# A hybrid four-layer trunk on one core: the state space layer's key units, B matrices and first value split moved

## The chip, the core and the metric

The program runs on one core of one Trainium2 chip, in one launch. The metric is the device time of a run in microseconds. TensorE is called PE here, VectorE DVE, ScalarE ACT and GpSimd POOL; SP starts most of the transfers. 256 tokens of width 1024 pass through four layers in float32.

## The reference, cut to what matters

```python
for i in range(4):
    hn = rms_norm(h, mix_norm_g[i])
    t = (pool_mixer, stick_breaking_attention, s5_mixer)[i % 3](hn, ...)
    h = h + t
    h = h + memory_cross_attention(rms_norm(h, xa_norm_g[i]), rms_norm(mem, mem_norm_g[i]), wq, wkv, wo)
    h = h + conv_glu_ffn(rms_norm(h, ffn_norm_g[i]), w_up, conv_w, conv_b, w_down)
return rms_norm(h, final_norm_g)

# s5_mixer, layer 2: 64 groups of 16 channels, 64 complex states each
bu = einsum('bcgi,gpi->bcgp', u, b_bar)           # B
x_t = a_bar * x_{t-1} + bu_t                      # recurrence over 256 tokens
y = gelu(real(einsum('bcgp,gip->bcgi', x, c_mat)) + d * u)
val, gate = split(y @ w_glu, 2); return val * sigmoid(gate)
```

The keys and values of the cross-attention come from `mem`, which does not depend on the layers before it. Their products can therefore be placed anywhere ahead of the cross-attention, and the kernel uses them as filler for PE.

## The kernel before

Every float32 product is three matmuls of split operands (`mm3`): a weight is loaded as 1 MB into one of three buffers called `raw`, ACT casts it into a high part `whi` and DVE or POOL subtracts to get the low part `wlo`, in two halves each (`load`). Each tag `whi` and `wlo` has six buffers. A program that lays the instructions out (the framework's scheduler) sets each engine's order within the order of the code and the limits given by `behind`; each engine then runs its own list strictly in order, and so do the DMA lists of SP, ACT and POOL.

The state space layer (`s5_mixer`, layer 2) runs between the FFN of layer 1 and the cross-attention of layer 2:

1. The normed tokens `u` are made on DVE (columns 0 to 511) and ACT (512 to 1023), then rearranged by eight SBUF to SBUF transfers into `uc` (L960).
2. `uc` is copied into `ur` (L985), transposed on PE (L989), and copied out as `v` (L990).
3. Four groups of small matmuls with the B matrices `bl` (1 MB each, `land(0)` to `land(3)`) give `S` (L1003, L1007). PE transposes `S`, and ACT and DVE copy the result into `SX` (L1027, L1029).
4. The recurrence runs on DVE alone over eight steps of chunks, `k` from 0 to 7, four instructions a step (L1049 to L1056), then three carried blocks (L1060 to L1066) that need the table `tab8`, which POOL computes.
5. PE adds the short-range part `taps_u` (four groups, matrices `tu`, L1076) and the carried part `carry` (four groups, matrices `ou`, L1101, needs the finished `X`), then GELU, a transpose and the GLU projection.

The filler is a plan: key units `k0` to `k3` (48 matmuls of 256 columns each, four key units in all) and the two value halves `v0` and `v1` (48 matmuls of 512 columns each), placed at named points by `fill`. A unit `+k1` only starts its load, `k1` multiplies. In the kernel before, `k1` and `k2` stand between step 1 and 2, `k3` after step 3, `v0` beside the recurrence, one group of `taps_u`, and then `v1`, whose PSUM banks are those of `v0` and come free when DVE has subtracted `vl` from them. The code puts that subtraction behind recurrence step 7 (`self.late = steps[7:8]`).

Of the kernel before, what the change touches and what calls it, by code (L numbers as in the profile page):

```python
# [36 lines left out]
class Trunk:  # L37
# [268 lines left out]
            return src[:, :, T * u : T * (u + 1)], DC, T  # L306
        return src[:, 4 * h : 4 * h + 4, D + 512 * u : D + 512 * (u + 1)], 4, 512

    def early(self, kind, l, u, **kw):

        for h in range(1 if kind == "k" else 2):
            self.loaded[kind, l, u, h] = self.load(*self.unit(kind, l, u, h), **kw)

    def weights(self, *key):
# [28 lines left out]
    def v_parts(self, l, nh):  # L343

        if nh == 0:
            self.V = self.kv_pair("v", TT, D)
        hi, lo = self.mg
        ps = [self.bank(), self.bank()]
        for kh in range(2):
            w = self.weights("v", l, nh, kh)  # L350
            for tt in range(TT):
                for k in range(4):
                    c = 4 * kh + k
                    s = slice(tt * P, (tt + 1) * P)
                    self.mm3(ps[tt][:], (hi[:, c, s], lo[:, c, s]), w(k, slice(0, 512)), c == 0, c == DC - 1)
                    yield
        vh, vl = self.V
        with self.behind(*self.late):
            for tt in range(TT):
                s = slice(512 * nh, 512 * (nh + 1))  # L360
                self.split(vh[:, tt, s], vl[:, tt, s], ps[tt][:])

    def fill(self, where):

# [11 lines left out]
    def plan(self, at, l, units):  # L376
        for u in units.split():
            if u[0] in "()":
                f = lambda u=u: self.portion(u, l)
            elif u[0] == "+":  # L380
                f = lambda u=u: self.early(u[1], l, int(u[2]), eng=self.nc.gpsimd if u[3:] else None)
            else:
                f = lambda u=u: (self.k_unit if u[0] == "k" else self.v_half)(l, int(u[1]))
            self.todo.setdefault(at, []).append(f)
# [547 lines left out]
    def s5_mixer(self, l, sp):  # L932
        nc, a = self.nc, self.a
        bls = []

        def land(mm):
            pool, tag = ((self.kv, "vh"), (self.kv, "vl"), (sp, "X"), (self.raw, "raw"))[mm]
            bl = pool.tile([P, 2, 4, 2, 2, 64], F32, tag=tag, name="bl")
            nc.sync.dma_start(bl[:].rearrange("p m q x r k -> p m (q x r k)"), self.blD[:, 2 * mm : 2 * mm + 2, :])
            bls.append(bl)  # L940

        land(0)
# [1 line left out]
        for tt in range(TT):  # L944
            rs.append(self.rstd(self.ss[tt]))
        self.fill("u0")
        u = self.big.tile([P, TT, D], F32, tag="xs", name="u")
        uc = sp.tile([P, 8, 16, 16], F32, name="uc")
        chain, firsts = [], []
        for tt in range(TT):  # L950
            r = rs[tt]
            firsts = []
            for nh, f in enumerate((nc.vector.tensor_scalar_mul, nc.scalar.mul)):
                s = slice(512 * nh, 512 * (nh + 1))
                done = f(u[:, tt, s], self.h[:, tt, s], r[:, 0:1])
                firsts.append(done.ins)

            for q in range(4):
                at = 32 * q + 16 * tt
                last = nc.sync.dma_start(  # L960
                    uc[at : at + 16].rearrange("c t a j -> c t (a j)"), u[:, tt, 256 * q : 256 * (q + 1)]
                )
        chain.append(done.ins)
# [3 lines left out]
        with self.behind(last.ins):  # L967
            for i, row in enumerate((a["s5_d"][0], a["mix_norm_g"][l])):
                nc.sync.dma_start(db[:, i, :], bass.AP(tensor=row.tensor, offset=row.offset, ap=[[256, 4], [0, 32], [1, 256]]))
            land(1)  # L970
            land(2)
        with self.behind(self.powed):
            nc.gpsimd.tensor_mul(db[:, 0, :], db[:, 0, :], db[:, 1, :])
            tab8 = self.s5_eighths(sp)
        self.late = firsts
        self.fill("u")
        land(3)
        self.after = [chain, chain + [last.ins]]
        self.fill("u1")
        self.late = ()  # L980
# [28 lines left out]
        tus = []  # L1009

        def taps_land(mm):
            pool, tag = ((self.acts, "ah"), (self.raw, "raw"), (self.raw, "raw"), (self.raw, "raw"))[mm]
            tu = pool.tile([P, 2, 2, 4, P], F32, tag=tag, name="tu")
            tus.append(tu)
            return nc.sync.dma_start(tu[:].rearrange("p r m q k -> p r (m q) k"), self.tD[mm]).ins
# [23 lines left out]
        with self.behind(last.ins):  # L1039
            nc.scalar.preload_act_table_set("gelu_apprx_tanh_and_others")  # L1040
        tab = sc[:, 0 : 3 * GP].rearrange("p (x g) -> p x g", g=GP)
        steps = []
        for k in range(8):
            nb = 4 if k < 7 else 3
            cur = lambda r=1: X[:, ::r, :, k : 8 * nb : 8].rearrange("p x g b -> p x b g")
            new = X[:, :, :, k + 1 : 8 * (nb - 1) + k + 2 : 8].rearrange("p x g b -> p x b g")
            add = SX[:, k : 8 * nb : 8].rearrange("p b x g -> p x b g")
            if k == 0:
                steps.append(vec.tensor_copy(new, add).ins)  # L1049
                continue  # L1050
            pr = two[:].rearrange("p (n x b g) -> p n x b g", n=2, x=2, b=4)[:, :, :, 0:nb]
            sh = [P, 2, nb, GP]
            vec.tensor_mul(pr[:, 0], cur(), tab[:, 0:1, :].unsqueeze(2).to_broadcast(sh))
            vec.tensor_mul(pr[:, 1], cur(-1), tab[:, 1:3, :].unsqueeze(2).to_broadcast(sh))
            vec.tensor_add(new, pr[:, 0], add)
            steps.append(vec.tensor_add(new, new, pr[:, 1]).ins)  # L1056
        for b in range(1, 4):
# [4 lines left out]
            for r, t in ((1, tab8[:, 0:1]), (-1, tab8[:, 1:3])):  # L1062
# [1 line left out]
                vec.tensor_mul(pr, carried[:, ::r].unsqueeze(3).to_broadcast(sh), t[:, :, :, 0:n].to_broadcast(sh) if r > 0 else t[:, :, :, 0:n])  # L1064
                new = X[:, :, :, 8 * b + 1 : 8 * b + 1 + n]
                steps.append(vec.tensor_add(new, new, pr).ins)  # L1066
        self.late = steps[7:8]
        self.fill("scan0")

        Y = self.accs()  # L1070

        def taps_u(mm):
            with self.behind(self.multiplied):
                for m, par, q in [(m, par, q) for m in (2 * mm, 2 * mm + 1) for par in range(2) for q in range(4)]:
                    c0 = (m % 4) * P
                    nc.tensor.matmul(  # L1076
                        Y[2 * par + m // 4][32 * q : 32 * q + 32, c0 : c0 + P], v[:, 2 * m + par, 32 * q : 32 * q + 32], tus[mm][:, par, m % 2, q, :],
                        start=m % 4 == 0, stop=False, tile_position=(0, 32 * q), skip_group_check=True,
                    )

        self.late = steps[-1:]
        taps_u(0)
        self.fill("scan1")
        self.late = ()
        for mm in (1, 2, 3):
            landed = taps_land(mm)
            taps_u(mm)

# [195 lines left out]
    def run(self, layers=range(DEPTH), parts="mcf"):  # L1284
# [14 lines left out]
        for l in layers:  # L1299
            if "c" not in parts:  # L1300
                break
            if l == first or l % 3 == 0 and l - 1 not in layers:
                self.plan((l, "start"), l, "k0 k1 k2 k3")
                self.plan((l, "pool"), l, "+v0g")
                self.plan((l, "xnorm0"), l, "(v0.8")
                self.plan((l, "xnorm"), l, ").5")
                self.plan((l, "xnorm1"), l, ")")
                self.plan((l, "soft"), l, "v1")
            elif l % 3 == 1:
                self.plan((l, "xnorm"), l, "k0 k1 k2 (k3.10")  # L1310
                self.plan((l, "xnorm1"), l, ")")
                self.plan((l, "soft"), l, "v0 v1")
            elif l % 3 == 2:
                self.plan((l - 1, "fnorm"), l, "(k0.10")
                self.plan((l - 1, "fnorm1"), l, ")")
                self.plan((l, "u0"), l, "+k1 +k2")
                self.plan((l, "u"), l, "k1 k2")
                self.plan((l, "u1"), l, "+k3")
                self.plan((l, "s"), l, "k3 +v0g")
                self.plan((l, "scan0"), l, "v0")  # L1320
                self.plan((l, "scan1"), l, "+v1g v1")
            else:
                self.plan((l - 1, "soft"), l, "k0")
                self.plan((l - 1, "fnorm"), l, "(k1.10")
                self.plan((l - 1, "fnorm1"), l, ")")
                self.plan((l, "mnorm"), l, "k2 k3")
                self.plan((l, "pool"), l, "+v0g")
                self.plan((l, "xnorm0"), l, "(v0.8")
                self.plan((l, "xnorm"), l, ").5")
                self.plan((l, "xnorm1"), l, ")")  # L1330
                self.plan((l, "soft"), l, "v1")
# [13 lines left out]
        for m in range(8):  # L1345
            at = (5 * m) // 2 + 2
            put((1, f"up{at}"), lambda m=m: self.s5_powers(m))
            put((1, f"up{at + 2}"), lambda m=m: self.s5_taps(m))
            if m % 2:
                put((1, f"up{at + 4}") if m < 7 else (2, "start"), lambda m=m: self.s5_spread(m // 2))  # L1350

        for l in layers:
            self.layer = l
# [64 lines left out]
```

## Time and profile before

| | us |
|---|---|
| median of three runs | 1495.98 (1493.38 to 1496.36) |
| the profiled execution | 1494.25 |
| its span, first to last instruction | 1492.5 |
| PE busy in the span | 1426.9 (96%) |
| DVE busy | 1093.6 (73%) |
| ACT busy | 839.8 (56%) |
| POOL busy | 127.2 (9%) |

PE's share is an average over the whole span. The chain that ended last gives PE 76%, DVE 11% and DMA 7%. The state space layer up to the start of its GLU lies between about 775 and 871 us of the span.

### The profile page before, as it was taken

Reading aid. Unit: us, or ns where it says so; the run is one execution under the profiler, and the core shown is the slowest. Engines: PE = TensorE matmul, PEld = TensorE weight load, DVE = VectorE, ACT = ScalarE, POOL = GpSimd, SP = SyncE. Lnnn points to the kernel's source line nnn. Section 1 sums busy time; section 2 is a strip of 40 time slices with the busy share of each in tenths; the row PEclk is TensorE's granted clock in tenths of the full one; section 3 lists DMA queues with packets and bytes.
Section 4 is the critical chain, followed back from the end, with each engine's and each line's share of the span. In section 5 each row is a group of like instructions: output and inputs, shape, how many; then the busy total and the mean of one; then the engine's idle time right before and its main releaser. Section 6 shows DMA issues by size and latency. Waiting matters only on the chain.

```text
span 1492.5 us, 25390 instructions
## 1 busy us (share of the span) xinstructions
PE 1426.9 (96%) x10354; PEld 1317.2 (88%) x10354; DVE 1093.6 (73%) x1720; ACT 839.8 (56%) x1351; POOL 127.2 (9%) x128
## 2 busy tenths in 40 slices
PE   7999999999999999999997679999999999999997
PEld 7897999988998989999986558999999999899996
DVE  6869887867886668978773646767767776677775
ACT  6654655547885556545544145656555565465553
POOL 3401000000000000101125100000000030000000
PEclk9999999999999999999998889999999999999999
DMA  7667656635444545766669383556555554465551
GB/s 253 229 166 222 221 202 204 215 127 190 142 150 156 198 149 197 233 218 227 220 192 275 139 270 130 172 170 219 170 188 180 174 204 145 142 225 171 182 185 43
DMA packets 205682, 279.75 MB, mean 187 GB/s; under 512 B 23740, under 2 KB 163132, under 8 KB 203644
## 3 DMA queue, kind: packets, MB, share of 16 engines
q1 hardware_dynamic: 199420, 263.08, 53.4%
q0 software_dynamic: 6144, 15.04, 3.1%
q8 instruction: 81, 1.33, 0.4%
q14 instruction: 37, 0.30, 0.1%
HBM read 264.24 MB, written 16.94 MB: 188 GB/s over the span
## 4 chain that ended last, share of the span: by engine, by line
PE 76%; DVE 11%; DMA 7%; ACT 3%; issue 2%; SPq 1%; POOL 0%; DVEq 0%; POOLq 0%; ACTq 0%
PE u L66 9%; PE u L67 9%; PE u L65 9%; PE mm L65 7%; PE mm L66 7%; PE mm L67 7%; PE acc L65 7%; PE acc L66 7%; PE acc L67 7%; DMA raw<-in_ffn_w_up_dram 3%; DVE wlo L71 3%; DVE ug L1256 1%; ACT whi L70 1%; DMA bl<-blD 1%; DVE h L434 1%
## 5 line engine op out<-in xcount | busy, mean ns | idle before, releaser
L71 DVE TENSOR_TENSOR wlo<-raw,whi 128x1024 fp32r<-128x1024 f32 x428 | 517.1, 1221 | 156.3 <-ACT whi L70 148.2
L70 ACT CAST whi<-raw 128x1024 fp32r<-128x1024 f32 (+1 forms) x450 | 460.0, 1045 | 192.6 <-DMA raw<-in_ffn_w_up_dram 58.2
L65 PE MATMUL u<-ah,whi 128*128 128x256 f32 x1408 | 400.3, 285 | 1.9 <-DVE ug L1256 1.4
L66 PE MATMUL u<-al,whi 128*128 128x256 f32 x1408 | 399.9, 284 | 0.7 <-DVE al L71 0.7
L67 PE MATMUL u<-ah,wlo 128*128 128x256 f32 x1408 | 399.6, 284 | 0.0
L65 PEld LDWEIGHTS u<-ah,whi 128*128 128x128 f32 x1408 | 271.1, 193 | 6.4 <-issue 2.8
L66 PEld LDWEIGHTS u<-al,whi 128*128 128x128 f32 x1408 | 271.3, 193 | 3.6 <-DVE al L71 1.1
L67 PEld LDWEIGHTS u<-ah,wlo 128*128 128x128 f32 x1408 | 271.3, 193 | 0.0
L1256 DVE SCALAR_TENSOR_TENSOR ug<-u,cwT,ug 128x255 f32<-128x255 f32 x352 | 168.6, 480 | 99.6 <-ACT ug L1254 94.4
L1254 ACT ACTIVATE ug<-u,cwT 128x256 f32<-128x256 f32 x176 | 99.0, 562 | 183.7 <-PE u L67 122.7
L65 PE MATMUL acc<-whi,gg 128*128 128x512 f32 x352 | 138.0, 392 | 0.0
L66 PE MATMUL acc<-wlo,gg 128*128 128x512 f32 x352 | 137.9, 392 | 0.0
L67 PE MATMUL acc<-whi,gg 128*128 128x512 f32 x352 | 136.9, 389 | 0.0
L66 PE MATMUL mm<-al,whi 128*128 128x256 f32 x384 | 109.3, 285 | 0.1
L65 PE MATMUL mm<-ah,whi 128*128 128x256 f32 x384 | 109.1, 284 | 0.0
L67 PE MATMUL mm<-ah,wlo 128*128 128x256 f32 x384 | 108.8, 283 | 0.0
L176 POOL TENSOR_TENSOR r<-v,mhalf 128x1 f32<-128x1 f32 x28 | 22.0, 788 | 826.8 <-DVE v L172 678.2
L67 PEld LDWEIGHTS acc<-whi,gg 128*128 128x128 f32 x352 | 66.1, 188 | 14.4
L65 PEld LDWEIGHTS acc<-whi,gg 128*128 128x128 f32 x352 | 66.4, 189 | 11.7
L66 PEld LDWEIGHTS acc<-wlo,gg 128*128 128x128 f32 x352 | 66.4, 189 | 10.7
L65 PE MATMUL acc<-whi,ah 128*128 128x512 f32 (+1 forms) x192 | 73.0, 380 | 1.9 <-ACT whi L70 1.7
L66 PEld LDWEIGHTS mm<-al,whi 128*128 128x128 f32 x384 | 73.9, 192 | 0.8 <-DVE al L71 0.6
(354 smaller groups left out, 2573.8 us busy)
## 6 DMA issues: line engine op xcount, KB each, us to landing
raw<-in_ffn_w_up_dram SPq DMA_DIRECT2D x88, 1024.0 KB
raw<-in_ffn_w_down_dram SPq DMA_DIRECT2D x44, 1024.0 KB
raw<-in_xa_wkv_dram SPq DMA_DIRECT2D x30, 1024.0 KB
raw<-in_xa_wq_dram SPq DMA_DIRECT2D x16, 1024.0 KB
raw<-in_xa_wo_dram SPq DMA_DIRECT2D x16, 1024.0 KB
raw<-in_sb_w_qkv_dram SPq DMA_DIRECT2D x12, 1024.0 KB
raw<-in_s_w_glu_dram SPq DMA_DIRECT2D x8, 1024.0 KB
raw<-in_sb_w_o_dram SPq DMA_DIRECT2D x4, 1024.0 KB
```

What stands on the lines that cost most here:

```text
L65: mm(out, lh, rh, start=start, stop=False)
L66: mm(out, lh, rl, start=False, stop=False)
L67: self.multiplied = mm(out, ll, rh, start=False, stop=stop).ins
L70: x = self.nc.scalar.copy(hi, src)
L71: y = (eng or self.nc.vector).tensor_sub(lo, src, hi.bitcast(F32))
L176: self.powed = nc.gpsimd.tensor_tensor(r[:], v[:], self.mhalf[:], ALU.pow).ins
L434: self.nc.vector.tensor_add(hs, hs, ps[:])
L1254: nc.scalar.activation(u[:, s, :], out, AF.Identity, bias=cw[3], scale=cw[2])
L1256: nc.vector.scalar_tensor_tensor(u[:, s, sh:], out[:, : T - sh], cw[2 - sh], u[:, s, sh:], ALU.mult, ALU.add)
```

## The change

`k3` is planned with `k1` and `k2`. B matrix 1 is loaded ahead of the tokens, and matrices 2 and 3 are started from POOL's list behind the two reciprocal roots `r`. Four of the eight `uc` transfers are started from ACT's list. The low part of the first half of `v0`'s weights goes from POOL to DVE. `taps_u(1)` is taken ahead of `v1`, with its matrix in a buffer of its own (tag `al`). `v0` is emitted inside the recurrence at `k == 7`, and the first multiply of step 7 is held behind the two `vl` subtractions. One scratch transfer (`s5_spread(3)`) is emitted later.

```diff
@@ early
+            kw.update({"eng": engs[h]} if engs else {})
@@ v_parts
-                self.split(vh[:, tt, s], vl[:, tt, s], ps[tt][:])
+                self.halved = self.split(vh[:, tt, s], vl[:, tt, s], ps[tt][:])[1:]
@@ s5_mixer
-        def land(mm):
+        def land(mm, eng=nc.sync):
-            nc.sync.dma_start(bl[:].rearrange("p m q x r k -> p m (q x r k)"), self.blD[:, 2 * mm : 2 * mm + 2, :])
+            eng.dma_start(bl[:].rearrange("p m q x r k -> p m (q x r k)"), self.blD[:, 2 * mm : 2 * mm + 2, :])
         self.fill("u0")
+        land(1)
-            for q in range(4):
+            for q in (2, 3, 0, 1):
-                last = nc.sync.dma_start(
+                last = (nc.sync if q < 2 else nc.scalar).dma_start(
-            land(1)
-            land(2)
         with self.behind(self.powed):
+            land(2, nc.gpsimd)
+            land(3, nc.gpsimd)
+            tab8 = self.s5_eighths(sp)
             nc.gpsimd.tensor_mul(db[:, 0, :], db[:, 0, :], db[:, 1, :])
-            tab8 = self.s5_eighths(sp)
         self.late = firsts
         self.fill("u")
-        land(3)
@@ taps_land
-            pool, tag = ((self.acts, "ah"), (self.raw, "raw"), (self.raw, "raw"), (self.raw, "raw"))[mm]
+            pool, tag = ((self.acts, "ah"), (self.acts, "al"), (self.raw, "raw"), (self.raw, "raw"))[mm]
@@ the recurrence
+            if k == 7:
+                self.fill("scan0")
+                half = self.halved
-            vec.tensor_mul(pr[:, 0], cur(), tab[:, 0:1, :].unsqueeze(2).to_broadcast(sh))
+            with self.behind(*half):
+                vec.tensor_mul(pr[:, 0], cur(), tab[:, 0:1, :].unsqueeze(2).to_broadcast(sh))
-        self.late = steps[7:8]
-        self.fill("scan0")
+        taps_land(1)
         self.late = steps[-1:]
         taps_u(0)
+        taps_u(1)
         self.fill("scan1")
-        for mm in (1, 2, 3):
+        for mm in (2, 3):
@@ the plan of layer 2
-                self.plan((l, "u0"), l, "+k1 +k2")
-                self.plan((l, "u"), l, "k1 k2")
-                self.plan((l, "u1"), l, "+k3")
-                self.plan((l, "s"), l, "k3 +v0g")
+                self.plan((l, "u0"), l, "+k1 +k2 +k3")
+                self.plan((l, "u"), l, "k1 k2 k3")
+                self.plan((l, "u1"), l, "+v0dg")
```

On DVE, inside the recurrence (steps 5 to 7; `vl` is the low part of the first value half, `two` and `X` are the recurrence), the kernel before has no subtraction here:

```order
L1056 TENSOR_TENSOR X<-X,two 128x2x4x32
L1053 TENSOR_TENSOR two<-X,sc 128x2x96
L1054 TENSOR_TENSOR two<-X,sc 128x2x96
L1055 TENSOR_TENSOR X<-two,SX 128x2x3x32
L1056 TENSOR_TENSOR X<-X,two 128x2x3x32
L1060 COPY sc<-X 128x64
L1064 TENSOR_TENSOR two<-sc,tab_8524 128x512
```

The changed kernel has both ahead of step 7:

```order
L71 TENSOR_TENSOR vl<-mm,vh 128x512
L1061 TENSOR_TENSOR X<-X,two 128x2x4x32
L1058 TENSOR_TENSOR two<-X,sc 128x256
L1059 TENSOR_TENSOR two<-X,sc 128x256
L1060 TENSOR_TENSOR X<-two,SX 128x2x4x32
L71 TENSOR_TENSOR vl<-mm,vh 128x512
L1061 TENSOR_TENSOR X<-X,two 128x2x4x32
L1058 TENSOR_TENSOR two<-X,sc 128x2x96
```

The two subtractions moved from the second carried block up into steps 5 and 6.

On ACT, from the tokens `u` on, the kernel before has this list (`kh` casts a key unit, `whi` a weight, `ur`, `v`, `S`, `SX` as in the steps above):

```order
L955 ACTIVATE u<-h,r 128x512 x2
L70 CAST kh<-mm 128x512 x2
L70 CAST whi<-raw 128x1024 x2
L985 COPY ur<-uc 128x512 x2
L990 COPY v<-mm 128x512 x2
L1007 COPY S<-mm 128x512 x2
L70 CAST whi<-raw 128x1024 x4
L70 CAST kh<-mm 128x512
L1029 COPY SX<-mm 128x8x32
```

In the changed kernel the same place reads:

```order
L957 ACTIVATE u<-h,r 128x512 x2
L962 DMA uc<-u 16x8x256 x4
L70 CAST kh<-mm 128x512 x3
L986 COPY ur<-uc 128x512 x2
L991 COPY v<-mm 128x512
L70 CAST whi<-raw 128x1024 x2
L991 COPY v<-mm 128x512
L1008 COPY S<-mm 128x512
L70 CAST whi<-raw 128x1024 x2
L1008 COPY S<-mm 128x512
L1030 COPY SX<-mm 128x8x32
```

The casts of the first value half's two weights moved from behind the two copies of `S` to between the copies of `v` and of `S`, and the third `kh` moved ahead of `ur`.

On PE, where the second value half begins, the kernel before has one group of taps and then a run on one bank, `mm_9013`, with twelve matmuls before the second bank `mm_9014`:

```order
L1076 MATMUL acc2_8975<-tu_8836,v_8662 32x128 x4
L65 MATMUL mm_9013<-whi_8995,mgh_6215 128x512
L66 MATMUL mm_9013<-wlo_8996,mgh_6215 128x512
L67 MATMUL mm_9013<-whi_8995,mgl_6216 128x512
L65 MATMUL mm_9013<-whi_8999,mgh_6215 128x512
```

The changed kernel has a second group of taps (`tu_8973`), and then both banks at once:

```order
L1080 MATMUL acc0_8975<-tu_8973,v_8733 32x128 x4
L1080 MATMUL acc2_8977<-tu_8973,v_8733 32x128 x4
L65 MATMUL mm_9031<-whi_9013,mgh_6215 128x512
L65 MATMUL mm_9032<-whi_9013,mgh_6215 128x512
L66 MATMUL mm_9031<-wlo_9014,mgh_6215 128x512
```

The second matmul of `v1` now writes the second bank, so it needs both subtractions `vl`, not only the first.

## Rows read from the trace of the kernel before

**Rows 1.** The page: the span, and the group of low-part subtractions on DVE.
```profile
span 1492.5 us, 25390 instructions
...
L71 DVE TENSOR_TENSOR wlo<-raw,whi 128x1024 fp32r<-128x1024 f32 x428 | 517.1, 1221 | 156.3 <-ACT whi L70 148.2
```

**Rows 2.** Waits of PE, 770 to 935 us: total us, times, longest.
```profile
PE mm L65 <- DVE vl L71: 11.5, 1, 11.5
PE acc L1101 <- DMA ou<-caD: 5.8, 2, 2.9
PE mm L989 <- ACT ur L985: 4.8, 1, 4.8
PE mm L1003 <- DMA bl<-blD: 3.9, 2, 2.5
```

**Rows 3.** Windows: engines' busy us, granted PE clock, DMA share, GB/s (the last three).
```profile
780.00:790.00 10.00, 6.55 (x55) 6.35 (x53) 3.23 (x4) 3.06 (x4) 5.33 (x11) 1.00 1.16 124
790.00:797.00 7.00, 5.54 (x48) 4.67 (x48) 2.66 (x5) 2.33 (x5) 0.00 (x0) 0.52 1.00 352
...
839.50:845.00 5.50, 5.49 (x13) 4.33 (x14) 5.21 (x9) 0.00 (x0) 0.00 (x0) 0.52 0.00 0
```

**Rows 4.** Timeline of PE from uc to v0: start, us, line, count [idle before].
```profile
791.37 3.67 PE L989 MATMUL mm<-ident,ur 128*128 128x128 f32 x16 [4.82 <-ACT ur L985]
...
799.40 1.08 PE L1003 MATMUL mm<-bl,v 128*32 128x128 f32 x32 [2.49 <-DMA bl<-blD]
801.92 3.64 PE L1003 MATMUL mm<-bl,v 128*32 128x128 f32 x64 [1.44 <-DMA bl<-blD]
...
812.12 1.47 PE L1027 MATMUL mm<-ident,S 128*128 128x128 f32 x12
...
815.56 1.01 PE L65 MATMUL mm<-whi,mgh 128*128 128x512 f32 x2 [0.83 <-ACT SX L1029]
```

**Rows 5.** Timeline of PE from the first taps to the GLU.
```profile
826.95 1.08 PE L1076 MATMUL acc<-tu,v 128*32 128x128 f32 x32
839.51 0.79 PE L65 MATMUL mm<-whi,mgh 128*128 128x512 f32 x1 [11.48 <-DVE vl L71]
...
855.83 1.35 PE L1101 MATMUL acc<-ou,X 64*32 64x128 f32 x64
860.03 1.16 PE L1101 MATMUL acc<-ou,X 64*32 64x128 f32 x64 [2.85 <-DMA ou<-caD]
864.13 3.67 PE L1101 MATMUL acc<-ou,X 64*32 64x128 f32 x128 [2.94 <-DMA ou<-caD]
...
870.93 0.50 PE L65 MATMUL mm<-whi,ah 128*128 128x512 f32 x1 [1.65 <-ACT ah L1121]
```

**Rows 6.** Timeline of DVE: the recurrence.
```profile
816.05 0.42 DVE L1049 COPY X<-SX 128x256 f32<-128x256 f32 x1 [0.68 <-ACT SX L1029]
...
831.20 0.59 DVE L1055 TENSOR_TENSOR X<-two,SX 128x256 f32<-128x256 f32 x1
...
838.77 0.68 DVE L71 TENSOR_TENSOR vl<-mm,vh 128x512 fp32r<-128x512 f32 x1
...
844.30 0.62 DVE L1066 TENSOR_TENSOR X<-X,two 128x448 f32<-128x448 f32 x1
```

**Rows 7.** Timeline of ACT: the uc copies, and the casts of v0's second weight.
```profile
790.70 1.14 ACT L985 COPY ur<-uc 128x512 f32<-128x512 f32 x2 [1.63 <-DMA uc<-u]
...
807.21 2.00 ACT L70 CAST whi<-raw 128x1024 fp32r<-128x1024 f32 x2 [0.69 <-DMA raw<-in_xa_wkv_dram]
```

**Rows 8.** Timeline of POOL: d times uc, and one low part.
```profile
799.13 4.51 POOL L992 TENSOR_TENSOR uc<-uc,db 128x2048 f32<-128x2048 f32 x1
...
805.64 2.39 POOL L71 TENSOR_TENSOR wlo<-raw,whi 128x1024 fp32r<-128x1024 f32 x1 [1.58 <-PE mm L1003]
```

**Rows 9.** Timeline of SP: the uc transfers, and v0's two weights.
```profile
778.04 5.45 SPq L960 DMA_DIRECT2D uc<-u  x8
...
786.47 4.45 SPq L88 DMA_DIRECT2D raw<-in_xa_wkv_dram  x2
```

More of the change, by code (lines that the diff above doesn't have):

```diff
@@ L307, in unit, with early @@
         return src[:, 4 * h : 4 * h + 4, D + 512 * u : D + 512 * (u + 1)], 4, 512
-    def early(self, kind, l, u, **kw):
+    def early(self, kind, l, u, engs=(), **kw):
         for h in range(1 if kind == "k" else 2):
+            kw.update({"eng": engs[h]} if engs else {})
             self.loaded[kind, l, u, h] = self.load(*self.unit(kind, l, u, h), **kw)
@@ L380, in plan @@
             elif u[0] == "+":
-                f = lambda u=u: self.early(u[1], l, int(u[2]), eng=self.nc.gpsimd if u[3:] else None)
+                f = lambda u=u: self.early(u[1], l, int(u[2]), engs=[None if c == "d" else self.nc.gpsimd for c in u[3:].replace("g", "gg")])
             else:
@@ L1041, in s5_mixer @@
         tab = sc[:, 0 : 3 * GP].rearrange("p (x g) -> p x g", g=GP)
-        steps = []
+        steps, half = [], ()
         for k in range(8):
@@ L1349, in run @@
             if m % 2:
-                put((1, f"up{at + 4}") if m < 7 else (2, "start"), lambda m=m: self.s5_spread(m // 2))
+                put((1, f"up{at + 4}") if m < 7 else (2, "u1"), lambda m=m: self.s5_spread(m // 2))
         for l in layers:
```

## The prediction

> **What bounds the kernel now.** The page comes first: in a span of 1492.5 us [rows 1] PE is busy 96%, so a time that goes must be a time in which PE waits. The list of PE's waits, cut to the state space layer, shows them: 11.5 us for `vl` on DVE, 5.8 us in two waits for `ou`, 4.8 us for the rearranged tokens, 3.9 us for `bl` [rows 2], 26.0 us together. The reader should then look at the clock in the windows: it is 0.52 (so mostly the lower level, 1.2 GHz) in 790 to 797 us and again in 839.5 to 845 us, both times directly behind one of these waits [rows 3]. So a long wait is paid twice, once as idle time and once in slow matmuls behind it. The timelines say which step holds the layer. From 791.37 us on it is one chain: transposes, B groups, `k3`, transposes of `S` from 812.12 us, and DVE's recurrence from 816.05 us [rows 4, 6]. I call that start of the recurrence R and count from it. PE does `v0` and one group of taps until 828.0 us (826.95 + 1.08), then waits for the first `vl`, which stands late in DVE's list, until 839.51 us, R + 23.5 [rows 5, 6]. The carried part starts at 855.83 us, R + 39.8, and the GLU at 870.93 us, R + 54.9 [rows 5]. Behind the GLU nothing in the change moves, so I take its start as the finish line: what it gains, the run gains.
>
> **Up to R.** `k3` goes ahead of the tokens' transposes. It removes the 6.6 us between the B groups' end (801.92 + 3.64 = 805.56 us) and 812.12 us [rows 4], and fills the wait of 4.82 us ahead of 791.37 us: `k1` and `k2`, twice as many matmuls, ran for 11.6 us up to 786.55 us (791.37 - 4.82), so `k3` takes 5.8 us and PE is busy to 792.4 us. Ahead of `u`, two more low parts of 1.22 us each [rows 1] stand in DVE's list, and two more casts of 1.0 us [rows 7] on ACT ahead of the norm's squares. They run side by side, so I put `u` 2.2 us later: its transfers start at about 780.2 us, not 778.04 us [rows 9].
>
> Then the transfers. Before, `uc` was first started at 778.04 us and had all landed at 790.70 us [rows 7, 9], with the DMA share at 1.16 but only 124 GB/s moved from 780 to 790 us [rows 3]. I read that as engines full with small pieces, about 9.5 us of work for `uc`. Starting half of them from ACT saves issue time (5.45 us for eight on SP [rows 9]; four on each side take 2.7 us), but the engines were already full, and the two B matrices that POOL now starts at the same moment add to their work. If two rings halved the time of `uc`, it would land at 786 us or so; that belongs to the quick case below. The Trainium skill speaks against that case, in "DMA: Bandwidth & Descriptors", section "Issuing engines are not separate DMA queues": transfers started from several engines end up on the same 16 DMA engines and interleave there, and only the issue time is saved. The share of 1.16 agrees with it; by that rule `uc` saves nothing beyond the 2.7 us of issue.
>
> So I sum the DMA work from 780.5 us: `uc` 9.5 us, then at 352 GB/s [rows 3] the two matrices (2.1 MB, 6.0 us), one scratch copy (0.5 MB, 1.5 us) and `v0`'s first weight (1.05 MB, 3.0 us): that weight lands at about 800.5 us. `uc` is somewhere within, at 791 to 795 us, and PE waits 1 to 3 us for it behind `k3`, not 4.8.
>
> The cost is in ACT's list: the two casts of that weight now stand between the first and the second copy of `v`, so the third B group waits for a weight that PE needs only ten microseconds later. Casts 2.0 us, copy 0.6 us: 803.1 us. Groups three and four took 3.64 us after a wait and will again [rows 4]: 806.8 us. The second weight's casts (landing near 803.5 us) fit in beside them. From the transposes of `S` to R it was 816.05 - 812.12 = 3.9 us [rows 4, 6]; I add 0.5 us for the low clock. **R = 811.2 us, 4.8 us earlier.** Bounds: 806.5 us, where no cast waits for its transfer (k units to 792.4, copies 0.6, transposes 3.7, four groups 1.1 each, 2.0 us of casts, 3.9 us), and 816 us or later, where the weight lands 5 us later than I sum. I take the value between, because 807.21 us, the landing of `v0`'s second weight before, is the nearest row [rows 7] and the sum of the work is nearly the same.
>
> **From R to the GLU.** The `vl` subtractions now stand in steps 5 and 6. PE's list has the second bank in its second matmul of `v1`, so the later `vl` counts. The instruction that it follows began at 831.20 us and took 0.59 us, R + 15.7 [rows 6]; the first `vl` ahead of it adds 0.6 us, instructions that run beside PE's work a little slower than this one 0.3 us (my estimate), and the second is 0.68 us [rows 6]: R + 17.3. PE finishes `v0` at R + 11 and two groups of taps (1.08 us each [rows 5]) at R + 13, so a wait of 4.3 us stays of the 11.5. It is about as long as the one ahead of 791.37 us, behind which the clock was low, so I keep `v1` at its old length: from 839.51 us to 855.83 us are 16.3 us, less three groups of taps at 1.08 us, 13.1 us. Two groups are left behind it, 2.2 us. The carried part can start at R + 32.6, not R + 39.8. DVE's recurrence itself ends as before, at R + 28.9 (844.30 + 0.62 us [rows 6]), since the subtractions were inside it then as well. So it is not the next bound.
>
> The carried part has four groups of 1.35 us. Before, two `ou` matrices waited for buffers that `taps_u` 1 and 2 held; now only one does, that of the third group of taps, free at R + 31.5. The first of the two late ones before came 6.3 us behind its buffer (second taps over at 855.83 - 2 x 1.08 = 853.7, use at 860.03 us [rows 5]). So: groups one and two until R + 35.3, wait to R + 37.8, groups three and four until R + 40.5, then as before 3.1 us to the GLU (870.93 - 864.13 - 3.67 us [rows 5]): R + 43.6 against R + 54.9. **Gain 11.3 us.** Bounds: with no low clock in `v1` (as `v0`, 826.95 - 815.56 = 11.4 us [rows 4, 5]) and an `ou` landing without a wait, 4.2 us more; with the recurrence held up by POOL, less. POOL's list is the one that got longer ahead of DVE's need. The table `tab8` now ends behind both weights' low parts (2.39 us each), `d * uc` (4.51 us) and `v1`'s four low parts [rows 8]: from the cast of `v0`'s second weight 6 x 2.4 + 4.5 + about 7 us of small work = 26 us, some 832 us, and DVE needs it at about R + 21.5 = 832.7 us. It just fits; each microsecond more moves the recurrence's end, which has 32.6 - 28.9 = 3.7 us of slack to PE.
>
> **Sum.** 4.8 + 11.3 = 16.1 us. Against the profiled execution, whose own time is 1494.25 us (the span and 1.75 us around it), that gives 1478.2 us. The median shown, 1495.98 us, is 1.7 us higher, 1479.9 us on that base; I say **1479 us**.
>
> **The rivals.**
>
> *Quick transfers.* `uc` and `v0`'s first weight land before they are asked for, `v1` runs at full clock, and the last `ou` is there in time. R = 806.5 (9.5 us gained), 11.3 and 4.2 us more: 25.0 us, 1469 us. For it: two rings may overlap the gaps of the small pieces. Against it: a share above 1 leaves little room.
>
> *The cast stall eats the first part.* ACT holds the third B group until a weight that lands 5 us later than I sum, R stays at 816 us, and only the second part is left: 1494.25 - 11.3 = 1483 us. For it: five transfers now crowd into the same ten microseconds. Against it: before, the same bytes were through at 807 us.
>
> *Given back.* The GLU's weights set the pace from there, since their buffers are freed by `tu` and `ou`, and the earlier start is waited for later: no change, 1492 to 1496 us. Against it: these buffers come free earlier by as much as the GLU starts earlier.
>
> *Slower.* If the large pieces from POOL's queue share the engines at the pace of the small ones, 124 GB/s [rows 3], then the 5 MB up to `v0`'s first weight last 40 us, it lands at 821 us, R becomes 832 us (10.7 us behind it, as in the forecast), and the GLU starts at 875.6 us, 4.7 us later: 1499 us. This turns the balance from the point at which the weight lands later than 816.5 us. For it: 10 us at that pace are in the trace. Against it: from 790 us on, with POOL's copies and the weights mixed, 352 GB/s were moved.
>
> **How the numbers follow.** Forecast (1474 to 1483 us) 0.50, quick transfers 0.18, cast stall 0.18, given back 0.06, slower 0.07, something else 0.01. The range that leaves out no more than 2 in 10 reaches from a little below the quick case to some way beyond the cast stall: 1468 to 1488 us; the forecast's own is 1474 to 1483 us. A measurement of this kernel tells 0.2% (3 us) from no change, as its three runs lie 3 us apart. Faster: 0.50 + 0.18 + 0.18 and a little of "given back", 0.87; same 0.06; slower 0.07.
>
> **What would show it.** PE's wait for `vl` should fall from 11.5 to about 4 us, the waits for `bl` should be gone, and one wait for `ou` of some 2.5 us should be left. R should lie at 807 to 814 us, with ACT waiting for `raw<-in_xa_wkv` between the two copies of `v`. DVE should show no wait for POOL at its first carried block; if it waits there by more than 4 us, the POOL estimate was wrong. If R has moved but the GLU's start has not, the step "R to the GLU" failed; if the GLU starts earlier and the time stays, "nothing behind it moves" failed.

## The result, and the profile after

The changed kernel takes **1481.02 us** (median of 4 runs, 1480.47 to 1482.43), the kernel before 1494.68 us in the same comparison: a ratio of 0.992, 95% interval 0.9901 to 0.9939. The forecast was 1479 us, its range 1468 to 1488 us. The profiled span fell from 1492.5 us [rows 1] to 1480.7 us, by 11.8 us; the medians lie 13.7 us apart.

The first view to read again is the list of PE's waits, 770 to 935 us (total us, times, longest):

```profile
PE mm L990 <- ACT ur L986: 5.2, 1, 5.2
PE mm L65 <- DVE vl L71: 4.4, 2, 2.4
PE acc L1106 <- DMA ou<-caD: 3.5, 1, 3.5
PE mm L65 <- ACT ah L1126: 3.1, 2, 1.7
PE mm L1004 <- ACT v L991: 2.2, 1, 2.2
PE acc L65 <- ACT whi L70: 1.6, 1, 1.6
...
PE acc L1106 <- issue: 0.4, 1, 0.4
```

Against [rows 2], `vl` fell from 11.5 to 4.4 us, `bl` is gone, `ou` fell from 5.8 to 3.5 us, with 0.4 us more ahead of the same matmuls for which the profile shows no releaser (`issue`). But the wait for the rearranged tokens is as long as before (5.2 us) although `k3` now fills 5.8 us ahead of it, and there is a new one for a copy of `v`. PE's timeline shows where these lie (start, us, count, idle before; x4, x19 and x43 count only what lies in a view's window); it answers to [rows 4, 5]:

```profile
775.16 0.28 PE L65 MATMUL mm<-mgh,whi 128*128 128x256 f32 x1
...
797.78 1.12 PE L990 MATMUL mm<-ident,ur 128*128 128x128 f32 x4 [5.18 <-ACT ur L986]
806.13 1.29 PE L1004 MATMUL mm<-bl,v 128*32 128x128 f32 x19 [2.21 <-ACT v L991]
...
830.90 0.80 PE L65 MATMUL mm<-whi,mgh 128*128 128x512 f32 x1 [2.44 <-DVE vl L71]
846.41 0.85 PE L1106 MATMUL acc<-ou,X 64*32 64x128 f32 x43
851.95 1.11 PE L1106 MATMUL acc<-ou,X 64*32 64x128 f32 x59 [3.50 <-DMA ou<-caD]
859.06 0.50 PE L65 MATMUL mm<-whi,ah 128*128 128x512 f32 x1 [1.68 <-ACT ah L1126]
```

The tokens' transposes start 6.4 us later than before, and yet R comes 2.7 us earlier, since `k3` and the waits for `bl` no longer lie behind them. On DVE, the recurrence (answering to [rows 6]) shows the two `vl` inside it, and `tab8`'s first use behind POOL's last step of it (both timelines: start, us, line):

```profile
813.35 1.22 DVE L1050 COPY X<-SX 128x256 f32<-128x256 f32 x1 [1.02 <-ACT SX L1030]
...
827.23 0.67 DVE L71 TENSOR_TENSOR vl<-mm,vh 128x512 fp32r<-128x512 f32 x1
830.17 0.68 DVE L71 TENSOR_TENSOR vl<-mm,vh 128x512 fp32r<-128x512 f32 x1
...
833.91 0.70 DVE L1069 TENSOR_TENSOR two<-sc,tab 128x512 f32<-128x512 f32 x1
```
```profile
832.42 0.87 POOL L930 TENSOR_SCALAR tab<-tab 128x256 f32<-128x256 f32 x1
```

The program is the same up to `k1`, but each profiled execution reaches it a little earlier or later (773 to 782 us). So executions are compared from the start of `k1` (774.88 us before, 775.16 us after), in stretches worked out from each trace. R is the start of the copy of `X`; "uc" runs from the first transfer's start to the copy that needs it. In `b_on_sp` and `best1x` that copy did not wait for `uc`, so theirs is only an upper bound. Each ratio is to the kernel before in the same comparison.

```
kernel         uc   k1 to R  R to GLU  k1 to GLU  GLU to end  median us, ratio to before
before       12.7     41.2     54.9      96.1       621.6     1494.7
after        16.9     38.2     45.7      83.9       621.6     1481.0  0.992
second_only  13.1     41.2     45.5      86.7       618.0     1484.3  0.993
first_only   18.0     36.2     50.8      87.0       620.0     1483.3  0.993
uc_on_sp     19.8     39.7     43.7      83.4       617.9     1481.1  0.992
b_on_sp     <12.9     35.5     46.9      82.5       617.5     1475.9  0.988
no_queues    16.9     36.2     46.0      82.2       616.4     1476.4  0.989
vl_k5        17.6     37.0     40.0      77.0       618.5     1475.6  0.990
ou_swap      17.0     36.6     45.2      81.8       619.2     1479.9  0.992
b_early      15.6     33.2     57.6      90.8       617.8     1488.9  0.998
b_early_x    15.0     35.3     44.0      79.3       618.8     1477.6  0.991
best3        14.9     33.4     52.5      85.9       620.4     1484.8  0.995
best3x       15.5     35.9     39.8      75.7       618.6     1472.6  0.988
best1x      <12.9     37.9     38.9      76.8       621.3     1475.0  0.990
```

Before against after, 12.1 us go ahead of the GLU and nothing behind it. Between the other kernels the stretch behind the GLU differs by up to 5 us, so differences of a few us between single profiles are read from the stretches, not from the span. Those 5 us lie within the GLU itself. The changed kernel has a wait of 1.6 us there for a cast weight (in the list above) and then a low clock; the kernel before has both too, `b_on_sp` and `no_queues` neither. Windows as in [rows 3], the changed kernel and then `b_on_sp`, each from about 14 us behind the GLU's start:

```profile
873.00:881.00 8.00, 6.29 (x15) 4.73 (x16) 4.36 (x4) 4.28 (x5) 0.00 (x0) 0.58 0.72 199
```
```profile
872.00:880.00 8.00, 7.07 (x31) 5.51 (x31) 3.33 (x3) 4.74 (x6) 0.00 (x0) 1.00 0.64 210
```

The stretch up to R varies as well. The changed kernel, `vl_k5` and `ou_swap` have the same list on PE up to R, and yet take 38.2, 37.0 and 36.6 us. Between the first and the last the clock makes the difference: the third and fourth B group took 3.55 us behind a wait of 2.2 us in the changed kernel, and 1.95 us behind one of 2.8 us in `ou_swap` (the same windows, in this order):

```profile
806.13:809.68 3.55, 3.55 (x65) 3.03 (x66) 1.50 (x2) 2.81 (x4) 2.10 (x1) 0.53 0.46 134
```
```profile
809.52:811.47 1.95, 1.95 (x65) 1.75 (x66) 1.51 (x2) 1.95 (x3) 0.49 (x1) 1.00 0.21 88
```

So a wait of 2 to 3 us is followed by the lower clock in one execution and not in another, and a difference of some 1.6 us up to R can't be told from this in single profiles.

### The profile page after: what moved, and what is told of

Read it like the earlier page. It is cut to its first block, busy times and chain, and to the rows that moved or that the text cites. A ratio compares the mean times of both kernels' runs of the same rounds, so it can differ in the third digit from the quotient of the medians.

```text
span 1480.7 us, 25386 instructions
## 1 busy us (share of the span) xinstructions
PE 1426.4 (96%) x10354; PEld 1316.4 (89%) x10354; DVE 1096.5 (74%) x1722; ACT 839.3 (57%) x1351; POOL 124.3 (8%) x128
## 4 chain that ended last, share of the span: by engine, by line
PE 79%; DVE 9%; DMA 6%; ACT 3%; issue 1%; POOL 0%; SPq 0%; DVEq 0%; POOLq 0%; ACTq 0%
PE u L66 10%; PE u L67 10%; PE u L65 10%; PE mm L66 7%; PE mm L65 7%; PE mm L67 7%; PE acc L65 7%; PE acc L66 7%; PE acc L67 7%; DMA raw<-in_ffn_w_up_dram 3%; DVE wlo L71 2%; DMA raw<-in_xa_wkv_dram 2%; ACT whi L70 1%; DVE ug L1261 1%; DMA raw<-in_s_w_glu_dram 1%
## 5 line engine op out<-in xcount | busy, mean ns | idle before, releaser
L176 POOL TENSOR_TENSOR r<-v,mhalf 128x1 f32<-128x1 f32 x28 | 22.7, 813 | 810.5 <-DVE v L172 678.7
L65 PEld LDWEIGHTS acc<-whi,gg 128*128 128x128 f32 x352 | 66.4, 189 | 11.7
L66 PEld LDWEIGHTS acc<-wlo,gg 128*128 128x128 f32 x352 | 66.4, 189 | 10.7
L65 PEld LDWEIGHTS mm<-ah,whi 128*128 128x128 f32 x384 | 74.6, 194 | 0.3 <-ACT ah L70 0.2
```

The lines of the kernel that those rows point to most:

```text
L65: mm(out, lh, rh, start=start, stop=False)
L66: mm(out, lh, rl, start=False, stop=False)
L176: self.powed = nc.gpsimd.tensor_tensor(r[:], v[:], self.mhalf[:], ALU.pow).ins
```

## The experiments

**The two parts apart.** `second_only` is the kernel before with the part on the recurrence (`halved`, `fill("scan0")` inside the loop, `taps_u(1)` ahead of `v1`); `first_only` is the changed kernel with that part undone.

> The kernel before with the second part of the change alone: both subtractions of vl ahead of the last step of the recurrence, and two groups of taps ahead of the second half of v. Theory (the two parts add up, and this is the larger one): R stays at 816 us, the wait for vl falls from 11.5 us to 4 to 5 us in two pieces, the GLU starts at R + 45.7 as in the changed kernel instead of R + 54.9, so 9.2 us are gained: 1485.5 us against 1494.7. Rival (the recurrence is held by POOL's table once its steps come earlier, or the gain needs the earlier R): R + 50 or more, 1490 us. Second rival (it is the whole effect): 1481 us.

> The changed kernel with the second part undone: k3 ahead of the tokens, the transfers of uc on two queues and two B matrices from POOL, but both subtractions of vl behind the recurrence's step as before. Theory (the parts add up): R at 813.4 us as in the changed kernel, the wait for vl back at 11 us, the GLU at R + 54.9 = 868.3 us, 2.7 us gained: 1492 us. Rival (the first part is worth more than R shows, since it changes clock and transfers behind R as well): 1488 us or less. Second rival (worth nothing by itself): 1494.7 us.

Measured 1484.3 us (interval of the ratio 0.9916 to 0.9945) and 1483.3 us (0.9921 to 0.9946). The second part did what was expected. The first was worth far more alone than the 2.7 us expected: its first rival holds by its number. From `k1` to the GLU the parts gain 9.4 and 9.1 us alone and 12.1 us together, so they overlap. The trace of `first_only` shows a part of why: its first `vl` stands directly behind the last step,

```profile
828.25 0.48 DVE L1057 TENSOR_TENSOR X<-X,two 128x192 f32<-128x192 f32 x1
828.65 0.68 DVE L71 TENSOR_TENSOR vl<-mm,vh 128x512 fp32r<-128x512 f32 x1
```

R + 19.6 us, while before it stood among the carried blocks, R + 22.7 us [rows 6]. The planner put it there by itself; that it did so because `v0`'s loads stand earlier is my reading, not shown. R to the GLU falls by 4.1 us: PE's wait for `vl` is 2.9 us shorter (8.6 us) and the waits for `ou` 1.2 us (4.6 us), both of which the second part would have shortened as well. Of the rest of the overlap, 2.0 us lie ahead of R, hardly more than that stretch varies by itself.

**The queues.** Three kernels: all of `uc` on SP (`uc_on_sp`), the third and fourth B matrix on SP behind `uc` (`b_on_sp`), and the change without any of its queue edits (`no_queues`: the second part and `k3`'s place alone, added to the kernel before).

```
uc_on_sp:   last = nc.sync.dma_start(            # was: (nc.sync if q < 2 else nc.scalar)
b_on_sp:    land(2); land(3) behind db's rows    # was: land(2, nc.gpsimd); land(3, nc.gpsimd)
no_queues:  (u0) +k1 +k2 +k3, (u) k1 k2 k3, (s) +v0g
```

> The changed kernel with all eight transfers of uc started by SP, as before the change. Theory (the DMA engines are shared by whatever is in flight, and the issuing queue saves only issue time): uc is there 0 to 3 us later than the 797.1 us of the changed kernel, so 1481 to 1484 us. Rival (splitting uc over two queues is what made it land 6.4 us later than before): uc is there at 791 us again, PE's wait of 5.2 us is gone, 1476 us.

> The changed kernel with the third and fourth B matrix started by SP again, directly behind its half of uc and the row of d, not by POOL at the same moment as uc. Theory (uc landed at 797.1 us and not at 790.7 us because these 2.1 MB went through the DMA engines beside it): uc is there at 788 to 791 us, before k3 ends at 792.6 us, PE's wait of 5.2 us falls below 1 us, the B matrices land by 798 us, R comes to 807 to 809 us, and the time to 1475 to 1477 us. ACT's casts of v0's weight also leave their place between the two copies of v. Rival (the queue of the B matrices doesn't matter, uc is late because of its split): uc at 796 us or later, R at 813 us, 1481 us.

> The change without its part on the queues: k3 ahead of the tokens and the second part as in the changed kernel, but all of uc, and the third and fourth B matrix behind it, on SP as before, and v0's weights loaded from the place they had. Theory (k3's place and the second part make the whole gain, and the queue edits cost 4 to 5 us by putting the B matrices beside uc): uc is there 17 to 19 us behind the end of the FFN, PE waits less than 2 us for it, the waits for bl come back with 2 to 4 us, R lies 35 to 36 us behind the end of the FFN instead of 38.2, and the time is 1475 to 1477 us. Rival (the queue edits earn what the waits for bl cost before): R at 38 to 40 us behind the end of the FFN, 1481 us or more. Second rival (POOL's list, in another order here, holds up the first copy of the recurrence): that copy lasts more than 2 us instead of 0.4, and its excess is added.

`b_on_sp`: 1475.9 us (0.9863 to 0.9891), the expected time. ACT's list shows that its `uc` was no longer waited for: the copy stands directly behind the cast of `k3`, which waited for PE.

```profile
793.10 0.59 ACT L70 CAST kh<-mm 128x512 fp32r<-128x512 f32 x1 [5.17 <-PE mm L67]
793.58 1.14 ACT L986 COPY ur<-uc 128x512 f32<-128x512 f32 x2
```

So `uc` took at most 12.9 us, and the B matrices beside it cost at least 4 us. How two queues compare with the 12.7 us of one queue before can't be read from this run. R came 2.7 us earlier, not 4 to 6, as 3.6 us of waits for `bl` came back, and from `k1` to the GLU only 1.4 us of the 5 are left: 4.1 us lie in the GLU, where the wait and the low clock shown above are gone. The expectation did not name that, and no run shows why. `uc_on_sp` ended at 1481.1 us (0.9903 to 0.9928), within what was expected. Its edit takes back the split alone, and its `uc` is 2.9 us slower, about what the split saves in issue time: SP's eight starts take 5.72 us, the halves 2.77 us on SP and 3.12 us on ACT. From one queue, with the B matrices beside it, `uc` took 19.8 us, 7.1 us more than before. `no_queues`: 1476.4 us (0.9871 to 0.9912), the expected time, but not by the expected way: its `uc` took 16.9 us with no B matrix on POOL. SP's timeline says what was in flight instead:

```profile
777.65 0.37 SPq L88 DMA_DIRECT2D raw<-in_xa_wkv_dram  x1
778.24 0.34 SPq L939 DMA_DIRECT2D bl<-blD  x1
780.61 7.39 SPq L960 DMA_DIRECT2D uc<-u  x8
```

Again 2.1 MB, `v0`'s weight and a B matrix, started 2.4 to 3 us ahead of `uc`, and again 4.2 us more than before (SP's eight starts also took 7.39 us, not 5.45 [rows 9]). So POOL's queue is not the cause: bytes that are in flight delay `uc`, from POOL in one kernel, from SP in the other. That weight was paid back: it came early, and the copies of `v` did not wait. R lies 2.0 us earlier than in the changed kernel; here too most of the gain, 5.2 us, lies in the GLU.

**Behind R.** `vl_k5` holds both `vl` in front of step 5 (`if k == 5:` for `if k == 7:`); `ou_swap` uses the fourth `ou` ahead of the third (`carry(3); done = carry(2)`).

> The changed kernel with both subtractions of vl held in front of step 5 of the recurrence instead of steps 6 and 7. Theory (PE's 4.4 us of waiting for vl is only their place in DVE's list, and the low clock behind that wait is its consequence): the wait falls below 1.5 us, the granted clock in the first 5 us of v1 stays above 0.9 instead of 0.50, v1 takes 11.4 us instead of 13.6, but the carried part then waits for the end of the recurrence at R + 29.7 us, so only 2.5 to 3.3 us reach the GLU: 1478 us against 1481. Rival (v1 is slow for another reason than the wait): it takes 13.6 us again and the gain is all of the wait, still about 1478, but with the clock low. Second rival (DVE's recurrence is stalled by its new place): no gain, 1481 us.

> The changed kernel with the fourth ou matrix used, and started by SP, ahead of the third. Theory (the third has to wait on SP for the buffer that the third group of taps frees, and the fourth, whose buffer is free early, stands in the queue behind it): one group more is done in the wait of 3.5 us, the end of the carried part comes 1.5 to 2.4 us earlier and the GLU with it: 1479 us against 1481. Rival (the GLU's start hangs on its weights or on the gelu of the second half, not on the last ou): the GLU starts at R + 45.7 us again, 1481 us.

`vl_k5`: 1475.6 us (0.9876 to 0.9913); this interval overlaps that of the changed kernel a little, so the stretches carry the reading. The wait fell to 0.3 us, and the clock followed. The windows of the first 5 us of `v1` (us, busy of PE, PEld, DVE, ACT, POOL, granted clock, DMA share, GB/s), in the changed kernel and in `vl_k5`:

```profile
830.90:836.00 5.10, 5.10 (x12) 4.08 (x13) 4.69 (x9) 0.00 (x0) 2.30 (x3) 0.50 0.85 318
```
```profile
826.50:831.50 5.00, 4.90 (x20) 3.84 (x21) 4.79 (x8) 0.00 (x0) 5.00 (x6) 1.00 0.57 198
```

`v1` takes 11.7 us (826.47 to 838.12) instead of 13.7 (830.90 to 844.60): behind 4.4 us of waiting, the lower level cost 2.0 us more. As expected, the carried part then waits for the recurrence:

```profile
PE acc L1106 <- DVE X L1071: 4.1, 1, 4.1
```

It starts at R + 30.5 us, 2.5 us earlier. Yet R to the GLU gained 5.7 us: the expectation missed that the late `ou` lands during this wait. The four carried groups took 6.0 us (844.11 to 850.09), not 9.1.

`ou_swap`: 1479.9 us (0.9905 to 0.9936), not to be told from the changed kernel. The carried part shrank by 0.9 us, the GLU came at R + 45.2 us instead of 45.7: the rival holds. Its chain of waits runs through the GLU's first weight, whose load starts when the last two groups of taps (L1080) end, and not through the last `ou`:

```profile
846.54 1.93 PE acc L1080 x64
848.48 7.83 DMA raw<-in_s_w_glu_dram
856.34 1.99 ACT whi L70 x2
858.33 1.91 ACT ah L1126 x2
860.28 0.80 PE mm L65
```

**B matrices ahead of uc, and a copy that lasted 14 us.** `b_early` calls `land(2)` and `land(3)` on SP directly behind `land(1)`; `best3` adds the edits of `vl_k5` and `ou_swap`.

> The changed kernel with the third and fourth B matrix started by SP ahead of uc, behind the first two, when the windows from 770 to 780 us show 0 to 5 GB/s moved. Theory (uc and v0's weight are late because 2.1 MB go beside them): uc is there 12 to 13 us after its start as before the change, so about 18 us behind the end of the FFN instead of 21.9, no wait for bl, v0's weight in time for its casts, R 31 to 33 us behind the end of the FFN instead of 38.2: 5 to 7 us, 1474 to 1476 us. Rival (POOL's table, which is ready only 0.6 us before DVE takes it in the changed kernel, becomes the bound when R comes earlier): DVE waits for POOL at the first carried block and no more than 2 to 3 us are left, 1478 us. Second rival (uc's time is its own, many small pieces): uc as late as now, 1481 us.

> The three edits together: B matrices started by SP ahead of uc, both vl ahead of step 5, the fourth ou ahead of the third. Theory (each takes another wait of PE's away): 6 + 2.5 + 2 us, 1470 to 1472 us. Rival (POOL's table becomes the bound): 1475 to 1478 us, with DVE waiting for POOL at the first carried block.

Measured 1488.9 us (0.9968 to 0.9991) and 1484.8 us (0.9935 to 0.9972): the first is slower than the changed kernel, the second by its median (the intervals just touch), against theory and rivals alike. `uc` took 15.6 and 14.9 us, not the 12 to 13 expected: SP started the fourth B matrix only at 781.13 us in `b_early`, behind `v0`'s weight at 780.57 us, so 2.1 MB again went 2.4 to 2.9 us ahead of `uc` (783.48 us). The start of the copy of `X` did come early, 33.2 us behind `k1`, but the copy itself lasted 14.21 us, not 0.42 [rows 6], beside this on POOL (`b_early`, DVE and then POOL):

```profile
811.68 14.21 DVE L1050 COPY X<-SX 128x256 f32<-128x256 f32 x1 [1.03 <-ACT SX L1030]
```
```profile
811.57 4.61 POOL L993 TENSOR_TENSOR uc<-uc,db 128x2048 f32<-128x2048 f32 x1
816.09 0.24 POOL L1035 MEMSET X<- 128x64 f32 x1
816.21 9.42 POOL L71 TENSOR_TENSOR wlo<-raw,whi 128x1024 fp32r<-128x1024 f32 x4
```

POOL worked without a break from 811.57 to 825.63 us, the copy ended at 825.89 us; in `best3` it took 14.21 us as well. To test it, that one copy goes to ACT, alone (`b_early_x`) and with the other edits (`best3x`). `best1x` has the B matrices on SP behind `uc`, ahead of `db`'s rows, and all other edits.

```
-                steps.append(vec.tensor_copy(new, add).ins)
+                steps.append(nc.scalar.copy(new, add).ins)
```

> The kernel with the B matrices ahead of uc, and the first copy of the recurrence (X from SX, SBUF to SBUF) on ACT instead of DVE; nothing else differs. In the run without this edit that copy lasted 14.21 us on DVE, from 811.68 us to 825.89 us, while POOL worked without a break from 811.57 us to 825.63 us; in the kernel before it took 0.42 us. Theory (this copy can't start while POOL's instructions follow one another): on ACT it takes 0.6 us, R comes out at once, the wait for vl falls from 16.3 us to 3 or 4 us, and 12 to 13 us are gained: 1476 us against 1489. Rival (DVE waited for something else, such as the buffer of X or POOL's zeroing of it, and ACT will wait for the same): the copy on ACT lasts or waits until 825 us as well, 1489 us. Second rival (POOL's run slows every instruction of the recurrence, not this one): a part of the 13 us only, 1482 us.

> All three edits and the first copy of the recurrence on ACT. Theory: the 14.21 us of the copy go, as above; then both vl are there when the second group of taps ends, v1 runs at full clock, and the carried part waits for the end of the recurrence only: 1484.8 less 12 to 14 us, 1470.5 to 1473 us. Rival (POOL's low parts of v1, now in one run of 9.4 us, come too late for PE): 1476 us or more, with PE waiting for POOL.

> The third and fourth B matrix on SP directly behind uc, both vl ahead of step 5, the fourth ou ahead of the third, and the first copy of the recurrence on ACT. Theory (the gains of the run with the B matrices on SP, 5 us below the changed kernel, and of the earlier vl, 5.4 us below it, add up since they lie on the two sides of R): 1470.5 us. Rival (they overlap as the two parts of the change did, because the planner moves other instructions when one of them is made): 1474 to 1475 us.

`b_early_x`: 1477.6 us (0.9892 to 0.9921), 11.3 us faster than `b_early` by one moved copy:

```profile
812.97 0.67 ACT L1050 COPY X<-SX 128x256 f32<-128x256 f32 x1
```

The recurrence's other instructions took 0.64 us each beside the same work of POOL, so only this one was held: both rivals fall. `best3x`: **1472.6 us** (0.9859 to 0.9893), as expected, the lowest median here and below both kernels; `b_on_sp` reaches the same ratio with one edit, though by a shorter GLU and not by a shorter way to it (82.5 us against 75.7). `best1x`: 1475.0 us (0.9876 to 0.9914; the profiled execution took 1481.95 us and reached `k1` late, at 782.2 us), the rival's number, though for a reason it did not name: `v0`'s weight came last of all transfers and PE waited 7.9 us for the `SX` copies behind its cast on ACT.

## Why the prediction was right, and which of its terms were off

The sign and the main mechanism held: the second part is worth 9.2 us of R to the GLU (forecast 11.3), the first 3.0 us up to R (forecast 4.8), and nothing was given back behind the GLU, whose start lies 621.6 us ahead of the end in both. Both parts gave about 2 us less than forecast, 12.1 us and not 16.1. That the time came within 2 us of the forecast is in part luck: the medians lie 13.7 us apart where the profiled executions lie 11.8, and those of the kernel before spread from 1489.56 to 1496.36 us. "Behind the GLU nothing moves" held for this pair, but not for `b_on_sp` and `no_queues`. Step by step:

- **The transfers** are the mis-sized term: PE's wait behind `k3` was 5.2 us, forecast 1 to 3, and `v0`'s first weight landed 3.1 us late, which is what moved R (next point). I took `uc`'s 9.5 us of work as first in line and the B matrices as behind it. They ran beside it; from 780 to 790 us the window now shows

```profile
780.00:790.00 10.00, 10.00 (x85) 10.00 (x85) 1.97 (x4) 1.90 (x3) 3.70 (x9) 1.00 0.86 255
```

  against 124 GB/s [rows 3], and `uc` took 16.9 us. This is the "slower" rival's mechanism at a smaller price. By the rule that I cited from the Trainium skill ("DMA: Bandwidth & Descriptors", "Issuing engines are not separate DMA queues") the split of `uc` over two queues saves issue time only; `uc_on_sp` agrees, where one queue took 2.9 us longer and the forecast had 2.7.
- **The cast stall** came as described, 2.2 us: the weight landed at 803.6 us, forecast 800.5. The chain of the changed kernel shows why it was later: SP could start it only behind `db`'s second row, which stood until a transfer of `uc` was through.

```profile
780.23 11.58 DMA uc<-u
791.83 0.58 SPq L971
792.52 11.06 DMA raw<-in_xa_wkv_dram
803.60 1.99 ACT whi L70 x2
```

- **R** came at 813.35 us (forecast 811.2, bounds 806.5 to 816). The weight came 3.1 us late, and from its landing to R it was 9.75 us, not 10.7. The terms listed for the lower bound add up to 807.0, not 806.5.
- **`vl`** was done at R + 17.5 us (forecast 17.3), PE waited 4.4 us for it (4.3), `v1` kept its low clock and took 13.7 us (13.1), and the carried part began at R + 33.1 us (32.6). These terms are right in sum, though 0.8 us of them went into something not forecast, the first copy of the recurrence (1.22 us, not 0.42). `vl_k5` shows that here clock and wait belong together.
- **POOL's `tab8`** was ready at 833.29 us, 0.6 us before DVE used it: "it just fits" was right, DVE did not wait.
- **From the carried part to the GLU** I forecast one wait for `ou` of 2.5 us and then 3.1 us. Measured: 3.5 and 0.4 us, and 3.6 us. `ou_swap` shows that here the GLU's first weight sets the start as well. It was started when the last taps ended (846.54 us) and cast from 855.12 us; so the mechanism of the rival "given back" is there in small, for some 0.5 us.

The forecast added its two parts. The runs show that such a sum is not safe: alone the parts gain some 18 us, together 12.1. Of the 6.4 us of overlap 4.1 lie behind R, where the planner moved a subtraction up by 3.1 us when only the part ahead of R was edited.

## What to carry to other kernels

A small-piece transfer on the critical path pays for large ones that are in flight beside it, here 3 to 7 us for 2.1 MB, from POOL's queue as from SP's: start the large ones early enough to be through, or behind it. A wait of PE is worth more than its length where the clock falls behind it; whether it does is looked up in the windows of the execution at hand. A start taken as finish line has to be checked against what comes behind it. And where a planner sets the order, look up after each edit where it put the instructions of the next stage, before adding gains.

## What was not expected of the hardware

A copy of 128x256 fp32 from SBUF to SBUF on DVE took 0.42 us with POOL idle, 1.22 us where it began beside a DMA issue of POOL, 1.71 us beside the end of a low part of `v0`, and 14.21 us beside six POOL instructions in an unbroken row. On ACT it took 0.67 us beside the same row. The Trainium skill ("SBUF — State Buffer", "Who interferes with whom") says that DVE's copies can compete with GpSimd for one pair of ports, where the later one is blocked until the other's instruction is over. The trace agrees that the copy is blocked; that it stays blocked through the next instructions as well is what the row of 14.21 us adds. But an unbroken row does not always hold it. In `no_queues` (DVE and then POOL) the copy began beside three low parts of about 2.4 us each and ended at 813.10 us, 0.3 us behind the first of them, while the next was running:

```profile
811.78 1.32 DVE L1049 COPY X<-SX 128x256 f32<-128x256 f32 x1 [1.81 <-ACT SX L1029]
```
```profile
810.47 7.11 POOL L71 TENSOR_TENSOR wlo<-raw,whi 128x1024 fp32r<-128x1024 f32 x3
```

In both runs in which it was held to the end it had begun 0.1 us behind the start of `d * uc` on POOL. Why DVE got in between two POOL instructions in one case and not in the other stays open.
